# A layer with seven-product projections: the SSD cut into small pieces, loads ahead of use, two sums kept in SBUF

## The chip, the cores and the metric

The kernel runs on one core of a Trainium2 chip. The metric is device time in microseconds (us), the median of several runs. Engine names are those of the profile: PE multiplies matrices, DVE works element by element, ACT computes functions and scaled copies, POOL is a second element-wise engine, and SP issues nearly all DMA transfers. Each engine works through its own list of instructions in order.

## The reference

One layer of a decoder trunk with two branches behind one input projection and ahead of one output projection. The gMLP branch multiplies u, a spatially mixed v and a SiLU gate; the SSD branch is a depthwise convolution and a chunked state-space scan.

```python
def hybrid_layer(x, pre_w, w_in, v_norm_w, v_norm_b, ws, bs, gmlp_norm_w,
                 conv_w, conv_b, dt_bias, a_log, d_skip, ssd_norm_w, w_out, post_w):
    h = rms_norm(x, pre_w)                                   # x: 2048 x 1024
    proj = jnp.einsum('bld,dc->blc', h, w_in)                # w_in: 1024 x 6160
    u, v, zg, z, xbc, dt_raw = jnp.split(proj, SPLITS, axis=-1)
    y_a = spatial_gating(u, v, zg, v_norm_w, v_norm_b, ws, bs, gmlp_norm_w)
    y_b = ssd_mixer(xbc, z, dt_raw, conv_w, conv_b, dt_bias, a_log, d_skip, ssd_norm_w)
    mixed = jnp.einsum('blc,cd->bld', jnp.concatenate([y_a, y_b], axis=-1), w_out)
    return x + rms_norm(mixed, post_w)
...
def ssd_mixer(xbc, z, dt_raw, conv_w, conv_b, dt_bias, a_log, d_skip, norm_w):
    xbc = jax.nn.silu(causal_depthwise_conv(xbc, conv_w, conv_b))   # width 4
    xs, bm, cm = jnp.split(xbc, [SSD_WIDTH, SSD_WIDTH + SSD_GROUPS * D_STATE], axis=-1)
    ...
    decay = jnp.exp(jnp.where(causal, seg, -jnp.inf))        # per chunk of 128 and head
    cb = jnp.einsum('bclgn,bcsgn->bclsg', cm, bm)
    y_diag = jnp.einsum('bclsg,bclsgr,bcsgrp->bclgrp', cb, decay, xdt)
    states = jnp.einsum('bclgn,bclgr,bclgrp->bcgrpn', bm, decay_to_end, xdt)
    ...                                                      # state from chunk to chunk
    y_off = jnp.einsum('bclgn,bcgrpn,bclgr->bclgrp', cm, prev_states, jnp.exp(da_cs))
    y = (y_diag + y_off + xs * d).reshape(bsz, seq, SSD_WIDTH).astype(z.dtype)
    return grouped_rms_norm(y * jax.nn.silu(z), norm_w, SSD_WIDTH // SSD_GROUPS)
```

All is float32, with one sequence of 2048 positions and width 1024.

## The kernel before

**Tiling.** The sequence is cut into four blocks b of 512 positions. The input projection runs as six units of 1024 output columns (z, the two halves of xbc, v, and two halves of u with its gate), the output projection as unit 6. A unit uses Strassen's scheme in Winograd's form: blocks pair up as (0, 2) and (1, 3) (`PAIRS`), and for a pair seven products P1 to P7 take the place of eight. P1, P2 and P4 have a plain piece of the activations as their A operand, the others a sum: S3 for P7, S2 for P6, and one in P5 and P3; the weights have such sums (t3, t) as B operands. A finished operand is a 128x1024 float32 tile r, split into a rounded high part by ACT (line 158) and a rest by DVE (line 159). Three passes over the parts make up one product (`mm3`, lines 163 to 165).

**Steps.** A step is one product, one pair and one half or quarter j of the inner dimension: 24 products of 128x512 on four accumulators `acc`. A unit has 28 steps (`SETS` says which products come together; each set goes through both pairs), unit 6 has 56 (`ONES`), 224 in all. After the last j of a product, `after` adds the accumulator into the results in hand (tiles u, c), and `use_...` hands a finished result on: z through SiLU to DRAM, xbc to DRAM as `raw`, v with statistics, u into the gating, the last one into the output norm. Unit 0 stores its split A sums (`a_d`); units 1 to 5 load them as they are.

**What sets the order.** `look_ahead(i)` makes the operands of the steps up to i+3: loads, sums and split in one go. All other work is written as tasks, generators that issue a piece and yield. `run_tasks` runs after each accumulator's products and advances one task that is due. `issue_after` ties the piece to the step's last product, so pieces fall between steps on each engine. The SSD is one such task from unit 1 on: 16 blocks (b, group g), each a convolution of four 128x512 tiles (ACT line 341, DVE line 343 three times each, ACT line 344 with SiLU), transposes to `xtok` and `btok`, and four chunks. A chunk needs its decay matrix E (a load, four Relu and an Exp on ACT, lines 366 to 371), the operand xdt (DVE line 414) and products y_ps and st_ps (lines 428 to 433), then sums on DVE and POOL. Its state goes on to the next chunk. In units 4 and 5 the gMLP gating (`spatial`, `gate_in`, `gate_out`) runs beside it. `bring` loads what the last half of a row block needs for its output.

**Places.** The r tiles are a pool of six, A operands four, B operands five, and SSD and result tiles share `gpool` of 30. The sums S2 and S3 of units 0 and 6 go through DRAM (`s_d`): the P6 step stores S3 from tile t, then overwrites t with S2 and stores that; P7 and P3 load them back:

```python
        if name == "P6":
            t, q, r = load([piece(0, 0), piece(1, 0), piece(1, 1)])
            tt(t, t, q, ALU.subtract)
            nc.sync.dma_start(out=s_d[v, p, "S3", j], in_=t)
            tt(t, r, t, ALU.subtract)
            nc.sync.dma_start(out=s_d[v, p, "S2", j], in_=t)
```

## Time and profile before

| | us |
|---|---|
| median of 3 runs | 1740.42 (1739.19 to 1742.76) |
| the profiled execution | 1746.94 |
| its span, first to last instruction | 1745.2 |
| PE busy in it | 1564.6 (90%) |
| DVE, ACT, POOL busy | 1137.4, 908.9, 390.5 |

The times of the rows below are microseconds from the start of the span of the profiled execution. A busy PE is a PE with a product under way, not one at its peak, so the pace of steps is read from the times at which they begin. A wait is put down to what ended last.

### The profile page before, as it was taken

What the parts mean: (1) busy time and instruction counts of PE and PEld (TensorE: products, weight loads), DVE (VectorE), ACT (ScalarE), POOL (GpSimd) and SP (SyncE); (2) the same over time, 40 slices, a digit from 0 to 9 for tenths busy, and PEclk for the clock granted to TensorE, in tenths of its full rate; (3) what the DMA queues carried; (4) which work ended last, traced back from release to release, by engine and by line L of the source; (5) the groups of instructions that cost most, each with busy time, mean ns of one, the idle gap of its engine ahead of it and who ended that gap; (6) DMA issues with size and microseconds to landing.
All of it is one profiled execution on the core that took longest, in us unless ns stands there. A gap on an engine that the chain in (4) does not pass through costs nothing.

```text
span 1745.2 us, 21775 instructions
## 1 busy us (share of the span) xinstructions
PE 1564.6 (90%) x7268; PEld 1292.8 (74%) x7268; DVE 1137.4 (65%) x1748; ACT 908.9 (52%) x1849; POOL 390.5 (22%) x441
## 2 busy tenths in 40 slices
PE   4987889899989999799998889897899999699897
PEld 3866678788777778587886777786678888578786
DVE  4347666555675758747897558686547835666886
ACT  4332245553565656656565656978736852232332
POOL 1000000033033225422334233443332310000021
PEclk9977899999989999799998999998999999899998
DMA  9699998877777677586775676464756557998797
GB/s 332 225 356 351 373 410 287 331 239 264 267 262 260 238 274 246 190 279 260 268 261 191 220 258 242 153 195 154 290 203 255 182 175 259 376 334 272 264 388 281
DMA packets 161424, 465.28 MB, mean 267 GB/s; under 512 B 19104, under 2 KB 35872, under 8 KB 149024
## 3 DMA queue, kind: packets, MB, share of 16 engines
q1 hardware_dynamic: 161312, 463.89, 74.7%
q8 instruction: 57, 0.93, 0.2%
q14 instruction: 55, 0.45, 0.1%
HBM read 354.64 MB, written 109.18 MB: 266 GB/s over the span
## 4 chain that ended last, share of the span: by engine, by line
PE 46%; DMA 22%; DVE 14%; ACT 10%; issue 4%; POOL 2%; SPq 1%; DVEq 0%; ACTq 0%; POOLq 0%
PE acc L163 13%; PE acc L164 13%; PE acc L165 13%; DMA r<-w_u 5%; DMA r<-yd 3%; DVE cv_out L343 3%; PE y_ps L428 2%; DMA E<-scr 2%; DVE a L159 2%; ACT E L370 1%; DMA cv_raw<-raw 1%; DMA hd<-h 1%; DMA a<-as0P 1%; PE s_ps L505 1%; ACT L371 1%
## 5 line engine op out<-in xcount | busy, mean ns | idle before, releaser
L163 PE MATMUL acc<-b,a 128*128 128x512 f32 x1344 | 545.3, 412 | 78.5 <-ACT b L158 34.6
L164 PE MATMUL acc<-b,a 128*128 128x512 f32 x1344 | 544.4, 406 | 0.2
L165 PE MATMUL acc<-b,a 128*128 128x512 f32 x1344 | 533.4, 403 | 2.7 <-DVE a L159 2.7
L163 PEld LDWEIGHTS acc<-b,a 128*128 128x128 f32 x1344 | 262.4, 196 | 142.1 <-ACT b L158 36.9
L165 PEld LDWEIGHTS acc<-b,a 128*128 128x128 f32 x1344 | 261.4, 195 | 60.7 <-DVE a L159 4.3
L164 PEld LDWEIGHTS acc<-b,a 128*128 128x128 f32 x1344 | 263.1, 196 | 55.9 <-DVE b L159 1.8
L158 ACT ACTIVATE a<-r 128x1024 fp32r<-128x1024 f32 x144 | 151.2, 1054 | 230.3 <-PE acc L165 99.1
L159 DVE TENSOR_TENSOR a<-r,a 128x1024 fp32r<-128x1024 f32 x144 | 178.7, 1243 | 98.3 <-ACT a L158 94.4
L163 PE MATMUL acc<-a,b 128*128 128x512 f32 x448 | 180.5, 406 | 10.7 <-DVE u L728 3.1
L343 DVE SCALAR_TENSOR_TENSOR cv_out<-cv_raw,cw,cv_out 128x512 f32<-128x512 f32 x192 | 163.4, 865 | 29.2 <-ACT cv_out L341 27.6
L164 PE MATMUL acc<-a,b 128*128 128x512 f32 x448 | 179.4, 400 | 0.0
L165 PE MATMUL acc<-a,b 128*128 128x512 f32 x448 | 179.0, 401 | 0.0
L159 DVE TENSOR_TENSOR b<-r,b 128x1024 fp32r<-128x1024 f32 x112 | 139.4, 1247 | 54.9 <-ACT b L158 54.9
L158 ACT ACTIVATE b<-r 128x1024 fp32r<-128x1024 f32 x112 | 117.6, 1052 | 106.0 <-PE acc L165 38.7
L182 ACT ACTIVATE junk<-y 128x128 bf16<-128x128 f32 (+1 forms) x192 | 65.2, 340 | 127.6 <-POOL y L445 118.6
L416 POOL TENSOR_TENSOR xde<-xtok,dte 128x256 f32<-128x256 f32 x64 | 52.4, 818 | 315.8 <-ACT xtok L390 315.8
L163 PEld LDWEIGHTS acc<-a,b 128*128 128x128 f32 x448 | 85.9, 192 | 30.6 <-DVE u L728 3.5
L437 POOL TENSOR_TENSOR state<-state,ex 128x256 f32<-128x256 f32 x60 | 49.7, 828 | 258.4 <-PE y_ps L431 258.4
L370 ACT ACTIVATE E<-E,cs 128x128 f32<-128x128 f32 x256 | 79.4, 390 | 41.4 <-DMA E<-scr 38.7
L165 PEld LDWEIGHTS acc<-a,b 128*128 128x128 f32 x448 | 86.2, 192 | 18.2
L164 PEld LDWEIGHTS acc<-a,b 128*128 128x128 f32 x448 | 86.2, 192 | 17.5
L171 POOL TENSOR_TENSOR o_r<-o_ms,mhalf 128x1 f32<-128x1 f32 x16 | 16.9, 1059 | 318.7 <-DVE o_ms L169 290.2
(146 smaller groups left out, 2189.5 us busy)
## 6 DMA issues: line engine op xcount, KB each, us to landing
r<-w_u SPq DMA_DIRECT2D x108, 512.0 KB, 5.2
r<-hd SPq DMA_DIRECT2D x96, 512.0 KB, 5.9
a<-as0P SPq DMA_DIRECT2D x40, 1024.0 KB, 6.5
a<-as1P SPq DMA_DIRECT2D x40, 1024.0 KB, 7.0
r<-yd SPq DMA_DIRECT2D x72, 512.0 KB, 5.1
r<-w_o SPq DMA_DIRECT2D x44, 512.0 KB, 5.3
E<-scr SPq DMA_DIRECT2D x64, 256.0 KB, 5.3
yd<-yT SPq DMA_DIRECT2D x64, 256.0 KB, 2.8
```

Of the source, the lines that this page charges most:

```text
L158: nc.scalar.activation(w[:, :, 0, :], t, AF.Copy)
L159: nc.vector.tensor_tensor(w[:, :, 1, :], t, w[:, :, 0, :], ALU.subtract)
L163: nc.tensor.matmul(dst, lhsT=a_hi, rhs=b_hi, start=first, stop=False, skip_group_check=True)
L164: nc.tensor.matmul(dst, lhsT=a_hi, rhs=b_lo, start=False, stop=False, skip_group_check=True)
L165: return nc.tensor.matmul(dst, lhsT=a_lo, rhs=b_hi, start=False, stop=last, skip_group_check=True)
L182: nc.scalar.activation(junk[:, 0:n], src, AF.Square, accum_out=dst)
L343: nc.vector.scalar_tensor_tensor(cv, raw[:, j:j + T], cw[:, ti, j:j + 1], cv, ALU.mult, ALU.add)
L370: nc.scalar.activation(E[:, h, :], E[:, h, :], AF.Relu, scale=-1.0, bias=d["cs"][:, o + h:o + h + 1])
L371: nc.scalar.activation(E, E, AF.Exp, scale=-1.0)
L416: nc.gpsimd.tensor_tensor(h4(xde[:, :]), xc, hv(d["dte"], g, c), ALU.mult)
L428: nc.tensor.matmul(yps[:, h * HD:(h + 1) * HD], lhsT=E[:, h, :], rhs=xdt[:, h * HD:(h + 1) * HD], start=True, stop=True)
L437: nc.gpsimd.tensor_tensor(h4(st[:, :]), h4(st[:, :]), ev(d["ex"], 1, g, c), ALU.mult)
```

## The change

- **SSD pieces.** A class `Ssd` holds one block's tiles, and its methods are small pieces. While one block's chunks run, the next block's convolution goes one tile at a time between them, and the results of the block before are transposed and stored. Loads of raw, E and zs are issued at least one piece ahead of the piece that uses them. The task starts a few products into unit 1, rather than in its sixth step. With many tasks due, `run_tasks` advances more than one. `spatial` loads v a piece ahead too.
- **Loads ahead.** `make_a` and `make_b` are generators: the first part loads, one step ahead of the second, which sums and splits. This doesn't hold for the loads of the stored A operands and for the sums of unit 0. The A operands are made two steps ahead, from a pool of three; there are seven r and 32 g tiles.
- **S2 and S3.** In unit 0, S3 stays in its r tile until P7, and POOL copies S2 into two g tiles until P3. Unit 6 keeps its S2 and S3 in DRAM.
- **Orders.** Unit 0 is now the first half of xbc and unit 1 is z. In a unit P4 comes ahead of P5 and P3. In unit 6 the order is P1, P7, P2, P6, P4, P5, P3: P7 computes S3 and the weights' t3 and stores them, P6 loads them. P5 and P3 are now the products that finish a row's second half.

```diff
-LOOK_A = 3
+LOOK_A = 2
...
-SETS = (("P1", "P2"), ("P6", "P7"), ("P5", "P3"), ("P4",))
-ONES = tuple((m,) for m in PRODS)
+SETS = (("P1", "P2"), ("P6", "P7"), ("P4",), ("P5", "P3"))
+ONES = tuple((m,) for m in ("P1", "P7", "P2", "P6", "P4", "P5", "P3"))
...
-    apool = ctx.enter_context(tc.tile_pool(name="apool", bufs=4))
+    apool = ctx.enter_context(tc.tile_pool(name="apool", bufs=3))
-    rpool = ctx.enter_context(tc.tile_pool(name="rpool", bufs=6))
-    gpool = ctx.enter_context(tc.tile_pool(name="gpool", bufs=30))
+    rpool = ctx.enter_context(tc.tile_pool(name="rpool", bufs=7))
+    gpool = ctx.enter_context(tc.tile_pool(name="gpool", bufs=32))
...
-            advance(min(due, key=lambda t: t[0]))
+            for t in sorted(due, key=lambda t: t[0])[0:1 + len(due) // 4]:
+                advance(t)
...
+    def ssd_stream():
+        order = [(b, 2 * u + n) for u in range(2) for n in range(2) for b in range(NB)]
...
+        for n in range(len(order) + 1):
+            nxt = Ssd(*order[n + 1]) if n + 1 < len(order) else None
+            if nxt:
+                while not ready(nxt.b, nxt.g):
+                    yield 5
+            if cur:
+                while (cur.b, cur.g // 2) not in zs_in:
+                    yield 5
+                cur.load_e(0)
+                cur.load_e(1)
+                cur.tok_x(0)
+                yield 0
+                cur.tok_x(1)
+            if prev:
+                next(prev.out, None)
+            yield 0
+            if cur:
+                cur.tok_b()
+                cur.decay(0)
+                yield 0
...
+            for c in range(NT):
+                if nxt:
+                    nxt.conv(c)
+                    if c + 1 < NT:
+                        nxt.load_raw(c + 1)
+                if c + 2 < NT:
+                    cur.load_e(c + 2)
+                yield 0
+                if c + 1 < NT:
+                    cur.operands(c + 1)
+                cur.chunk(c)
+                if c + 2 < NT:
+                    cur.decay(c + 2)
+                    cur.load_z(c + 2)
+                yield 0
+            cur.norm()
+            yield 0
+            prev, cur = cur, nxt
...
-    UNITS = [(use_z(0), False, SETS, 2), (use_xbc(0), True, SETS, 2), (use_xbc(1), True, SETS, 2),
+    UNITS = [(use_xbc(0), True, SETS, 2), (use_z(0), False, SETS, 2), (use_xbc(1), True, SETS, 2),
...
     def make_a(u, p, name, j):
...
         if name in PLAIN_A:
-            return split(apool, "a", load([piece(*PLAIN_A[name])])[0])
+            t, = load([piece(*PLAIN_A[name])])
+            yield
+            yield split(apool, "a", t)
+            return
         if 0 < u < 6:
+            yield
             w = apool.tile([P, 2, 2, T], F32R, name="a")
             nc.sync.dma_start(out=w[:, :, :, :].bitcast(F32), in_=a_d[p][name, j][:, :, :, :])
...
+            if u == 0:
+                t, q, r = load([piece(0, 0), piece(1, 0), piece(1, 1)])
+                tt(t, t, q, ALU.subtract)
+                s3_in[p, j] = t
+                tt(r, r, t, ALU.subtract)
+                s2 = s2_in[p, j] = [gt("s2") for _ in range(2)]
+                for kk in range(2):
+                    nc.gpsimd.tensor_copy(s2[kk], r[:, kk, :])
+                t = r
+            else:
+                q, t = load([piece(1, 1), s_d[p, "S3", j]])
+                yield
+                tt(t, q, t, ALU.subtract)
+                nc.sync.dma_start(out=s_d[p, "S2", j], in_=t)
         elif name == "P7":
-            t, = load([s_d[v, p, "S3", j]])
+            if u == 0:
+                t = s3_in.pop((p, j))
+            else:
+                t, q = load([piece(0, 0), piece(1, 0)])
+                yield
+                tt(t, t, q, ALU.subtract)
+                nc.sync.dma_start(out=s_d[p, "S3", j], in_=t)
...
     def make_b(u, name, j):
...
+            else:
+                t, r = load([t3_d[j], piece(0, 0)])
+                yield
             tt(r, t, r, ALU.add)
             nc.sync.dma_start(out=t_d[u, j], in_=r)
...
                 t, q = load([piece(1, 1), piece(0, 1)])
+                yield
                 tt(t, t, q, ALU.subtract)
+                nc.sync.dma_start(out=t3_d[j], in_=t)
...
+        upto(2, i + LOOK_A, lambda *a: (load_a(*a) if looked[0] <= a[0] else None, do_a(*a),
+                                        looked.__setitem__(0, max(looked[0], a[0] + 1))))
+        upto(3, i + LOOK_B, lambda *a: (load_b(*a) if looked[1] <= a[0] else None, do_b(*a),
+                                        looked.__setitem__(1, max(looked[1], a[0] + 1))))
+        upto(0, i + LOOK_A + 1, load_a)
+        upto(1, i + LOOK_B + 1, load_b)
...
         elif name == "P6":
-            t["2"] = gt("u2")
-            tt(t["2"], t["3"], acc, ALU.add)
+            if alone:
+                t["2"] = t["1"]
+                tt(t["3"], t["3"], acc, ALU.add)
+            else:
+                t["2"] = gt("u2")
+            tt(t["2"], t["1"], acc, ALU.add)
...
-                spawn(ssd_stream(), 30)
+                spawn(ssd_stream(), 4)
...
-            if u == 6 and name in ("P3", "P4") and j == nj - 2:
-                bring(PAIRS[p][name == "P4"], c)
+            if u == 6 and name in ("P3", "P5") and j == nj - 2:
+                bring(PAIRS[p][name == "P5"], c)
```

On PE in unit 3, at the end of its fifth step. The rows are instructions in their order; acc are the steps' products, the others the small ones of the SSD. Before:

```order
L165 MATMUL acc_5536<-b_5489,a_5484 128x512
L428 MATMUL y_ps_5440<-xdt_5394,E_5218 128x64 x4
L431 MATMUL y_ps_5440<-state1_235,cv_out_5198 128x256
L433 MATMUL st_ps_5446<-xde_5396,btok_5307 128x256
L428 MATMUL y_ps_5513<-xdt_5467,E_5384 128x64 x4
L431 MATMUL y_ps_5513<-state1_235,cv_out_5198 128x256
L433 MATMUL st_ps_5519<-xde_5469,btok_5307 128x256
L428 MATMUL y_ps_5572<-xdt_5531,E_5457 128x64 x4
L431 MATMUL y_ps_5572<-state1_235,cv_out_5198 128x256
L433 MATMUL st_ps_5578<-xde_5533,btok_5307 128x256
L387 MATMUL xt_tp_5684<-ident_220,cv_out_5618 128x128 x2
L387 MATMUL xt_tp_5684<-ident_220,cv_out_5626 128x128 x2
```

Three chunks follow on one another there, and the next block's transposes behind them. On PE at a chunk in the same unit after the change:

```order
L166 MATMUL acc_5935<-b_5428,a_5780 128x512
L427 MATMUL y_ps_5818<-xdt_5743,E_5649 128x64 x4
L430 MATMUL y_ps_5818<-state1_231,cv_out_5382 128x256
L432 MATMUL st_ps_5824<-xde_5745,btok_5529 128x256
L164 MATMUL acc_5935<-b_5428,a_5780 128x512
L165 MATMUL acc_5935<-b_5428,a_5780 128x512
L166 MATMUL acc_5935<-b_5428,a_5780 128x512
```

A chunk now stands alone between the steps' products, and some 20 to 35 products lie between it and the next.

On SP's queue in unit 0, where the first P6 operands are made; r are loaded pieces, w_u the weights, hd and h the normalised input, zs1 the results of z. Before:

```order
L151 DMA r_774<-w_u 128x1024
L151 DMA r_776<-w_u 128x1024
L642 DMA s00S30_118<-r_758 128x1024
L248 DMA h_800<-x_t 128x1024
L151 DMA r_867<-hd0_1_85 128x1024
L555 DMA zs1_157<-stage_992 128x512
L555 DMA zs1_157<-stage_1001 128x512
L555 DMA zs1_157<-stage_1023 128x512
L671 DMA t00_140<-r_776 128x1024
L555 DMA zs1_157<-stage_1032 128x512
L644 DMA s00S20_116<-r_758 128x1024
```

The stores of S3 and S2 stand among the loads, the second behind the first. After:

```order
L152 DMA r_770<-w_u 128x1024
L250 DMA h_788<-x_t 128x1024
L152 DMA r_855<-hd0_0_84 128x1024
L152 DMA r_857<-hd2_0_92 128x1024
L152 DMA r_859<-hd2_2_94 128x1024
L771 DMA t01_137<-r_770 128x1024
L254 DMA hd2_3_95<-h_788 128x1024
L250 DMA h_906<-x_t 128x1024
L152 DMA r_961<-hd0_1_85 128x1024
L152 DMA r_963<-hd2_1_93 128x1024
L152 DMA r_965<-hd2_3_95 128x1024
```

The stores are gone from there; the loads for the weights' sums now stand ahead of the loads for S3 and S2.

On SP's queue in unit 6, the first P6 step before; yd are the branches' outputs, w_o the weights:

```order
L151 DMA r_12306<-yd0_4_184 128x1024
L151 DMA r_12308<-yd2_4_200 128x1024
L151 DMA r_12310<-yd2_0_196 128x1024
L642 DMA s60S30_128<-r_12306 128x1024
L151 DMA r_12319<-w_o 128x1024
L644 DMA s60S20_124<-r_12306 128x1024
L151 DMA r_12321<-w_o 128x1024
L151 DMA r_12323<-w_o 128x1024
```

And the first P7 step after the change, which now computes S3:

```order
L152 DMA r_12018<-yd0_4_180 128x1024
L152 DMA r_12020<-yd2_4_196 128x1024
L152 DMA r_12022<-w_o 128x1024
L528 DMA yd3_3_203<-yT_11876 128x512
L152 DMA r_12024<-w_o 128x1024
L733 DMA s0S30_120<-r_12018 128x1024
L152 DMA r_12060<-yd0_5_181 128x1024
```

Six loads and two of the step's stores became four loads and one store here, with the loads of the next step right behind.

## Rows read from the trace of the kernel before

**Rows 1.** The first part of the page: busy time, share of the span and instructions of each engine.

```profile
PE 1564.6 (90%) x7268; PEld 1292.8 (74%) x7268; DVE 1137.4 (65%) x1748; ACT 908.9 (52%) x1849; POOL 390.5 (22%) x441
```

**Rows 2.** The table of stretches, cut at the start of units 0 to 6. Columns: from:to, length, then busy us (and instructions) of PE, PE weight loads, DVE, ACT and POOL, mean granted clock, DMA share, GB/s.

```profile
42.00:280.60 238.60, 209.05 (x907) 169.92 (x908) 143.17 (x240) 88.27 (x134) 2.01 (x2) 0.89 0.91 343
280.60:464.20 183.60, 177.70 (x827) 147.18 (x826) 106.70 (x151) 86.82 (x146) 32.99 (x40) 0.98 0.78 274
464.20:683.50 219.30, 201.14 (x963) 166.82 (x962) 147.24 (x215) 134.15 (x245) 67.99 (x79) 0.96 0.73 256
683.50:905.10 221.60, 205.68 (x983) 170.50 (x982) 158.24 (x250) 128.60 (x242) 76.65 (x87) 0.95 0.72 251
905.10:1159.80 254.70, 225.80 (x1104) 187.80 (x1104) 175.85 (x304) 168.34 (x402) 99.44 (x112) 0.93 0.62 211
1159.80:1395.20 235.40, 212.23 (x1065) 177.38 (x1064) 155.05 (x266) 168.10 (x461) 82.75 (x90) 0.95 0.63 217
1395.20:1733.90 338.70, 316.98 (x1361) 258.93 (x1359) 225.39 (x272) 114.90 (x181) 19.36 (x17) 0.96 0.83 297
```

**Rows 3.** The same view, of two undisturbed stretches: eight steps of P7 in unit 6, and three steps with three chunks in unit 2.

```profile
1440.70:1484.20 43.50, 43.50 (x194) 36.02 (x193) 24.91 (x25) 12.60 (x18) 0.00 (x0) 1.00 0.75 262
605.50:627.20 21.70, 21.70 (x110) 18.48 (x108) 15.30 (x26) 5.65 (x12) 9.17 (x13) 1.00 0.83 311
```

**Rows 4.** The timeline, unit 0: start, length, engine, line, operation, count.

```profile
64.97 3.64 PE L256 MATMUL dt_ps<-wdt,h 128*128 128x16 f32 x32
```

**Rows 5.** The table of stretches, the first ten steps of units 1 to 5.

```profile
280.60:345.90 65.30, 60.37 (x262) 49.07 (x260) 32.91 (x39) 34.21 (x52) 4.16 (x3) 0.95 0.81 297
464.20:549.90 85.70, 73.67 (x345) 60.06 (x344) 52.59 (x71) 55.15 (x100) 23.00 (x27) 0.94 0.68 236
683.50:782.60 99.10, 85.29 (x394) 70.01 (x392) 60.19 (x89) 55.35 (x107) 37.30 (x43) 0.88 0.69 233
905.10:1011.40 106.30, 89.59 (x425) 73.96 (x424) 72.71 (x124) 63.46 (x141) 44.61 (x51) 0.89 0.65 219
1159.80:1268.50 108.70, 86.91 (x430) 71.54 (x428) 69.97 (x114) 89.85 (x235) 42.35 (x45) 0.91 0.64 220
```

**Rows 6.** The waits between 280 and 1395 us: who waited for what, us in total, times, the longest.

```profile
ACT cv_out L341 <- DMA cv_raw<-raw: 62.3, 24, 6.4
...
ACT E L370 <- DMA E<-scr: 38.7, 18, 5.3
...
PE y_ps L428 <- DVE xdt L414: 12.4, 5, 6.3
...
PE acc L163 <- DMA a<-as0P: 8.2, 4, 5.7
```

**Rows 7.** The timeline in unit 3; in brackets the idle time before and what ended it.

```profile
709.29 2.45 ACT L370 ACTIVATE E<-E,cs 128x128 f32<-128x128 f32 x8 [4.05 <-DMA E<-scr]
...
712.46 1.28 ACT L371 ACT_TABLE_LOAD   x1
713.76 1.15 ACT L371 ACTIVATE E<-E 128x512 f32<-128x512 f32 x2
...
724.20 3.08 DVE L343 SCALAR_TENSOR_TENSOR cv_out<-cv_raw,cw,cv_out 128x512 f32<-128x512 f32 x4
...
727.86 0.41 DVE L414 TENSOR_TENSOR xdt<-xtok,dt 128x256 f32<-128x256 f32 x1
...
728.42 1.94 PE L428 MATMUL y_ps<-xdt,E 128*128 128x64 f32 x8 [6.34 <-DVE xdt L414]
```

**Rows 8.** The table of stretches in unit 6: the eight P6 steps, the first P5 step of the second pair, and the last sixteen steps (P3 and P4).

```profile
1484.20:1552.10 67.90, 50.79 (x194) 39.72 (x193) 43.03 (x43) 15.18 (x21) 0.00 (x0) 0.87 0.96 360
1617.90:1630.30 12.40, 7.96 (x26) 6.05 (x25) 8.83 (x14) 3.68 (x10) 0.00 (x0) 0.73 0.64 219
1645.00:1734.00 89.00, 88.94 (x393) 73.31 (x391) 72.93 (x119) 30.57 (x55) 13.54 (x12) 1.00 0.95 353
```

**Rows 9.** The DMA view of unit 0 (42 to 280.6 us): the sum, and by tensor the count, KB each, us from issue to landing.

```profile
DMA packets 23819, 81.91 MB, mean 343 GB/s; under 512 B 2672, under 2 KB 3184, under 8 KB 21756
...
r<-s00S SPq DMA_DIRECT2D x4, 512.0 KB, 7.6
```

**Rows 10.** The timeline of the start.

```profile
34.43 5.36 SPq L151 DMA_DIRECT2D r<-w_u  x4
...
41.95 2.08 PE L163 MATMUL acc<-b,a 128*128 128x512 f32 x4 [10.44 <-ACT b L158]
```

**Rows 11.** The groups of instructions: line, engine, operation, count, busy us, mean ns, idle before.

```profile
L343 DVE SCALAR_TENSOR_TENSOR cv_out<-cv_raw,cw,cv_out 128x512 f32<-128x512 f32 x192 | 163.4, 865 | 29.2 <-ACT cv_out L341 27.6
```

**Rows 12.** The chain of waits in unit 6, in order of time: start, us, what.

```profile
1447.31 1.24 DVE r L641
...
1448.93 5.50 DMA s60S<-r
```

**Rows 13.** The DMA view of the whole span: the loads of the finished A operands.

```profile
a<-as0P SPq DMA_DIRECT2D x40, 1024.0 KB, 6.5
a<-as1P SPq DMA_DIRECT2D x40, 1024.0 KB, 7.0
```

**Rows 14.** The waits of SP's DMA queue between 280 and 1395 us.

```profile
SPq L635 <- PE acc L165: 168.1, 59, 12.3
```

More of the change, by code (lines that the diff above doesn't have):

```diff
@@ L328, in hybrid_kernel, with __init__, load_raw @@
     raw_in = set()
-    def conv(b, g, res):
-        for i in range(4):
-            ti = (2 * g, 2 * g + 1, 8 + g, 12 + g)[i]
-            raw = gfull("cv_raw")
+    zs_in = set()
+    class Ssd:
+        def __init__(self, b, g):
+            self.b, self.g, self.d = b, g, dts.get(b)
+            self.raw, self.cv, self.E, self.zs, self.ops, self.xtok, self.y = {}, {}, {}, {}, {}, {}, {}
+        def load_raw(self, i):
+            b, g = self.b, self.g
+            raw = self.raw[i] = gfull("cv_raw")
             if b:
@@ L413, in operands @@
+        def operands(self, c):
+            g, d = self.g, dts[self.b]
+            E = self.E[c]
+            nc.vector.tensor_tensor(E, E, self.cbm[:, c, :].unsqueeze(1).broadcast_to([P, HG, P]), ALU.mult)
+            xc = h4(self.xtok[c])
             xdt = qt("xdt")
@@ L418, in operands, with chunk @@
             nc.gpsimd.tensor_tensor(xc, xc, dsk, ALU.mult)
-            return E, xdt, xde
-        ops = operands(0)
-        yield 5
-        for c in range(NT):
-            E, xdt, xde = ops
+            self.ops[c] = xdt, xde
+        def chunk(self, c):
+            b, g, d, cT, st = self.b, self.g, dts[self.b], self.cv[3], state[self.g % 2]
+            xdt, xde = self.ops.pop(c)
+            E = self.E.pop(c)
             first = b == 0 and c == 0
@@ L721, in after @@
                 o = gt("c11")
[L722 removed]
+                tt(o, t["1"], acc, ALU.add)
                 use(m1, 0, c, o, False)
```

239 lines of the change are left out of this document (133 added, 106 removed).

## The prediction, made before the result was known

> **What bounds the kernel now.** The page's busy times come first [rows 1]: PE is busy 90% of the span, so the question is what keeps it from its pace. The table by unit [rows 2] cuts the span where units begin (each 672nd matrix product on acc). Then the pace: eight steps with nothing among them run in 43.5 us, 5.44 each; three steps with three SSD chunks among them take 21.7, so a chunk is (21.7 − 16.32)/3 = 1.79 [rows 3]; the other small products take 3.64/32 = 0.114 [rows 4]. A unit of 28 steps should take 152.3 us plus its small products (in the program's order 8, 16, 16, 16, 8 chunks and 60, 100, 120, 240, 296 others in units 1 to 5: 21.1, 40.0, 42.3, 56.0, 48.0 us). What lies above that is lost, most of it as PE waiting, the rest as a clock below 1.00: 10.2, 27.0, 27.0, 46.4 and 35.1 us in units 1 to 5 (145.7), 57 in unit 0 (29 us of small products there), 32.3 in unit 6 (304.6 + 1.8). The three kinds of unit lose for different reasons.
>
> Unit 0 is full of transfers: DMA share 0.91 at 343 GB/s [rows 2]. In units 1 to 5 the share is 0.62 to 0.78; there the first ten steps (P1 and P2, whose after-work hands two results per pair on while the B operands of a new unit are split) lose 8.6, 17.1, 23.7, 27.3, 31.1 us, by the same pace with 2.3, 14.2, 21.0, 24.6, 23.2 us of small products [rows 5]: 107.8 of the 145.7. The other 90 steps lose 37.9, or 0.42 each. In these stretches DVE is busy 50 to 68% of the time, ACT up to 83%: they are not full on average, but work comes in clumps. The waits say the same [rows 6]: PE waits little for any one thing (12.4 for xdt, 8.2 for an A load), while ACT, in order, stands 62.3 us for conv input and 38.7 for E, loads issued in the very piece that uses them; behind them on ACT's queue stand splits and evictions. One such place [rows 7]: ACT waits 4.05 for E at 709; four conv steps run on DVE from 724.20 to 727.28 ahead of xdt at 727.86, and PE waits 6.34 for it. Unit 6 loses 24.4 of its 32.3 in the eight P6 steps (67.9 against 43.5, DMA share 0.96) and 7 in one P5 step of 12.4 us [rows 8].
>
> **The change part by part.**
>
> Unit 0. S2 and S3 in SBUF remove 16 transfers of 512 KB (a store and a load of each, two pairs, two j) = 8.4 MB of 81.9 [rows 9]; at 343 GB/s 24 us. The wait of the second P6 subtraction for the S3 store goes too. Eight POOL copies come in; POOL is busy 2.01 us of 238.6 there, so they hide; without that cover they would cost some 9 us, at the 19.36/17 of a POOL instruction in unit 6 [rows 2]. Next late is the rest of the traffic (73.5 MB), and the share can't rise far over 0.91. If something else sets the unit's length, 0; at the 0.96 that unit 6's P6 reaches, 73.5 MB take 203 us, −35. I take three quarters of the 24: −18 (0 to −35).
>
> Start. SP issues four hd loads and behind them, from 34.43, the four w_u loads, 1.34 us each; PE's first product waits for the first B split and starts at 41.95 [rows 10]. Now the first w_u load goes right behind the first hd load, three issues or 4.0 us sooner, but the other A splits, ahead of it before, still have to be made: −3 (0 to −4).
>
> Units 1 to 5. Nothing here leaves the engines; it moves. On PE one chunk comes with each step where three chunks and eight transposes stood together; on DVE three conv steps between two chunks where twelve went, in two pieces, ahead of a block; loads of raw, E and zs one piece ahead, which takes up to 62.3 + 38.7 us of ACT's waits. Then a good stretch's rate should hold: the 30 opening steps of units 1 to 3 lose 49.4, at 0.42 each 12.6, so −37. In units 4 and 5 the same steps carry the spatial gating as well, DVE 72.7 and 70.0 us of work against 79.0 and 77.6 of PE's own, nine tenths: a queue that full can't absorb peaks, and I take half of their 58.4: −29. A loads now have one buffer less and two steps' lead in place of three, and SP meets them after more loads issued ahead: +4 (0 to the rival below). Together −62, between 0 and −88.
>
> Two costs for ACT and DVE. Mixing Silu of conv with Exp of decay piece by piece raises the table loads in ACT's order from 72 to 86. The row shows 1.28 us for one, and the next Exp starts 0.02 us behind it [rows 7]: 14 × 1.28 = 18 us on an engine busy 52%, spread over 1100 us, a wait for PE only where ACT is late; I put it inside the half of units 4 and 5. The Trainium skill ("ScalarE: Activation LUTs", What ACT_TABLE_LOAD costs) speaks against such an order: a switch of sets costs 1283 ns and a drain of some 1380 ns, 2.66 us. The row agrees on the load; of a drain this place shows none. By the page the 14 switches would be an estimated 37 us of ACT, still off the path by the busy share. Second, conv steps now run beside the chunks' POOL work. Four of them in a row take 3.08, 0.77 each, the mean of all 192 is 865 ns [rows 7, 11]. If that excess of 0.095 doubled, DVE would get 192 × 0.095 = 18 us more. The Trainium skill ("SBUF — State Buffer", Who interferes with whom) gives a reason: a DVE operation with two SBUF inputs and a GpSimd one lock each other out of a shared port. The rows fit that without showing it; what it adds is inside the range.
>
> Unit 6. Before, a P6 step loads three A pieces and stores S3 and S2, for the first pair it also loads three B pieces and stores t, and the second subtraction waits for the S3 store: 5.50 us from 1448.93 [rows 12]. That is 56 transfers, 29.4 MB. Now P7 and P6 have 18.9 MB each: 52.5 us at 360 GB/s against 43.5, with loads a step ahead in seven r tiles hiding half or more of the 9; I lose 4 in each: 24.4 to 8, −16. At the end P5 and P3 both carry final output: with 44 A and B loads (23.1 MB) where P3 and P4 had 36 (18.9). 353 GB/s over 89 us moved 31.4 MB [rows 8]; 4.2 more at 372 (353/0.95) make 95.5 us against 87: +8. Small rest −1. Sum −9, between +10 (P5 and P3 lose 20, DVE busy 72.9 of 89 there) and −20.
>
> Sum: −18 − 3 − 62 − 9 = −92. The profiled execution took 1746.94 (span 1745.2), 6.5 over the median of 1740.42; the losses are differences within it, and off the median the sum gives **1648**.
>
> **The rivals.**
>
> Units 1 to 5 gain nothing (0.20). The stalls come from DVE and ACT being too full in the opening steps, not from the clumps, or the tiles for loads ahead run short: the 32 g tiles must now hold one block's conv input and output beside the other's E, xtok, cbm and four to eight results, so a load ahead waits on SP for a tile and the rest of SP's queue behind it. For it: nine tenths of DVE in units 4 and 5. Against it: units 1 to 3, where DVE had 32.9 us of work against 56.7 and PE lost 8.6 all the same. Then 1648 + 62 = 1710.
>
> Slower: A operands come late (0.12). Three A buffers: a load may go out when the operand three steps back is used up, leaving two steps, 10.9 us, for SP to reach it and the transfer to land. Landing takes 6.5 to 7.0 [rows 13]; SP already waited 168.1 us in 59 pieces for such a buffer, up to 12.3 [rows 14], and everything issued behind it (E, raw, B halves) waits too. Before, with three steps, 4 of the 40 loads of as0P made PE wait, by up to 5.7 [rows 6, 13]. If every fourth of the 80 is late by 5.7, 20 × 5.7 = 114: 1648 + 114 = 1762. It decides from 92/5.7, about 16 late loads of all 80. Against it: 4 us of slack, and two steps become 14.5 with chunks.
>
> All of it works better (0.08): units 4 and 5 reach the good rate as well (58.4 to 8.4: another −21), unit 0 the full −24, unit 6 its −20: 1648 − 21 − 6 − 11 = 1610; if some of the 0.42 a step goes too, 1595.
>
> **How the numbers follow.** 0.60 for the forecast, spread by its bounds over some 1620 to 1685, 0.20 for 1710, 0.12 for late A operands, 0.08 for the best case. The range 1595 to 1722 takes in all but the slower rival and some tails. Faster by over 0.2% (3.5 us, about what a measurement of this kernel can tell from no change): 0.60 + 0.20 + 0.08 less some for cases between 1710 and 1740 that slip: 0.86. Within: 0.03. Slower: 0.11.
>
> **What would show it.** Unit 0 about 220 us long with 73.5 MB and the same share; its length unchanged at a lower share would say that compute or a buffer bounds it. The ten opening steps of units 1 to 3 losing about 4 us each, of 4 and 5 about 15; ACT's waits for cv_raw and E by DMA gone; xdt no longer a wait of several us on PE. If the late-A rival holds, PE's waits for `a<-as` stand first in the table and SP's for PE's acc grow. Unit 6: P7 and P6 about 47 us each, no wait of a subtraction for a store, P5 and P3 together about 95. The prediction is wrong where units 1 to 5 keep their losses though ACT's waits for loads are gone, since then a full queue, not a late load or a clump, set them.

## The result and the profile after

| | before | after |
|---|---|---|
| median, us | 1741.51 (1739.19 to 1742.76, 4 runs) | 1664.1 (1660.53 to 1670.95, 4 runs) |
| ratio to before | | 0.9562 (95% interval 0.9526 to 0.9597) |
| span of the profiled execution | 1745.2 | 1669.2 |

The kernel is 4.4% faster, 16 us slower than the 1648 that was forecast and inside the range. The table of stretches of the changed kernel, units 0 to 6, answers to [rows 2], with the same columns:

```profile
37.00:247.60 210.60, 199.70 (x907) 164.61 (x908) 142.48 (x250) 70.21 (x108) 7.19 (x10) 0.92 0.91 347
247.60:444.00 196.40, 187.75 (x891) 154.99 (x890) 131.42 (x187) 125.36 (x215) 47.86 (x58) 0.98 0.81 282
444.00:667.50 223.50, 204.62 (x990) 169.21 (x989) 146.37 (x222) 145.58 (x267) 75.83 (x89) 0.96 0.75 254
667.50:879.90 212.40, 201.29 (x969) 166.69 (x968) 158.36 (x254) 133.25 (x237) 66.15 (x79) 0.97 0.77 264
879.90:1104.30 224.40, 207.88 (x1040) 173.33 (x1039) 159.47 (x269) 162.70 (x372) 84.95 (x89) 0.97 0.66 225
1104.30:1345.90 241.60, 217.69 (x1053) 180.77 (x1052) 144.23 (x253) 160.21 (x448) 82.32 (x92) 0.91 0.60 205
1345.90:1656.50 310.60, 308.77 (x1361) 253.00 (x1359) 224.65 (x274) 114.68 (x179) 20.60 (x17) 1.00 0.89 321
```

Against the rows of before, unit 0 is 28.0 us shorter, the start 5.0 (42.0 to 37.0), units 1 to 5 together 16.3 (1114.6 to 1098.3), unit 6 28.1, and the tail behind it 1.4 longer: 76.0, all of the span's difference. Forecast were 18, 3, 62 and 9. The total came out within 16 us, its terms did not: units 1 to 5 gave a quarter of their share, unit 6 three times its own. So that the total lies near the forecast is in part luck: units 1 to 5 fell short by 46, and the other three terms gave 31 more than was forecast.

The opening ten steps of units 1 to 5 answer to [rows 5]:

```profile
247.60:308.60 61.00, 60.48 (x284) 49.87 (x283) 43.41 (x52) 36.24 (x57) 11.85 (x12) 1.00 0.90 311
444.00:539.60 95.60, 81.58 (x380) 65.87 (x378) 57.95 (x84) 66.25 (x121) 32.23 (x37) 0.91 0.68 224
667.50:750.30 82.80, 75.70 (x364) 61.79 (x363) 57.82 (x84) 55.04 (x95) 25.29 (x28) 0.96 0.73 247
879.90:976.30 96.40, 80.54 (x399) 65.75 (x397) 65.08 (x110) 65.42 (x151) 43.31 (x44) 0.96 0.64 220
1104.30:1228.40 124.10, 100.19 (x477) 81.95 (x475) 74.56 (x126) 95.08 (x258) 59.15 (x67) 0.85 0.60 203
```

By the prediction's count (5.44 us a step, 1.79 a chunk, 0.114 for another small product) they lose 1.2, 22.5, 11.6, 21.5 and 39.2 us: 96.0, where it was 107.8. The last row matters most: a clock of 0.85 over 124 us. The waits between 247 and 1346 us, against [rows 6]:

```profile
ACT cv_out L355 <- DMA cv_raw<-raw: 70.0, 34, 5.4
...
ACT E L371 <- DMA E<-scr: 31.7, 16, 6.9
...
PE acc L164 <- DMA a<-as1P: 11.9, 3, 9.8
...
PE y_ps L427 <- DVE E L410: 7.6, 3, 4.0
...
PE acc L164 <- DMA a<-as0P: 2.9, 4, 1.4
```

ACT still waits for raw and E, 101.7 us in all, where it was 101.0: issuing a load one piece ahead didn't shorten these waits in sum. A loads made PE wait 14.8 us in 7 places, not in twenty.

The products of unit 6, in the order P1, P7, P2, P6, P4, P5, P3, against [rows 8]:

```profile
1391.40:1436.40 45.00, 44.39 (x193) 35.77 (x192) 26.77 (x27) 15.07 (x17) 0.00 (x0) 1.00 0.87 324
...
1480.00:1523.50 43.50, 43.50 (x194) 36.02 (x193) 35.81 (x40) 14.55 (x20) 0.00 (x0) 1.00 0.99 372
...
1567.00:1611.10 44.10, 44.02 (x194) 35.82 (x193) 36.25 (x50) 16.83 (x27) 5.19 (x3) 1.00 0.95 345
1611.10:1656.50 45.40, 44.26 (x193) 35.68 (x191) 44.74 (x76) 14.19 (x26) 9.13 (x9) 1.00 1.03 390
```

P7, P6, P5 and P3 (the four rows) run at 45.0, 43.5, 44.1 and 45.4 us: PE never waits long, while the transfers reach 372 and 390 GB/s.

### The profile page after: what moved, and what is told of

Same layout as the page of the kernel before. It is cut to its first block, busy times and chain, and to the rows that moved or that the text cites. A ratio compares the mean times of both kernels' runs of the same rounds, so it can differ in the third digit from the quotient of the medians.

```text
span 1669.2 us, 21722 instructions
## 1 busy us (share of the span) xinstructions
PE 1543.6 (92%) x7268; PEld 1276.9 (76%) x7268; DVE 1129.3 (68%) x1756; ACT 929.3 (56%) x1863; POOL 394.5 (24%) x449
## 5 line engine op out<-in xcount | busy, mean ns | idle before, releaser
L164 PE MATMUL acc<-b,a 128*128 128x512 f32 x1344 | 544.4, 405 | 32.0 <-DMA a<-as1P 11.9
L165 PE MATMUL acc<-b,a 128*128 128x512 f32 x1344 | 534.6, 398 | 0.0
L166 PE MATMUL acc<-b,a 128*128 128x512 f32 x1344 | 526.1, 398 | 2.5 <-DVE a L160 1.7
L164 PEld LDWEIGHTS acc<-b,a 128*128 128x128 f32 x1344 | 257.0, 191 | 91.7 <-DMA a<-as1P 13.2
L166 PEld LDWEIGHTS acc<-b,a 128*128 128x128 f32 x1344 | 256.5, 191 | 60.0 <-DVE a L160 4.6
L165 PEld LDWEIGHTS acc<-b,a 128*128 128x128 f32 x1344 | 257.5, 192 | 51.0
L164 PE MATMUL acc<-a,b 128*128 128x512 f32 x448 | 182.4, 416 | 18.6 <-ACT a L159 4.7
L165 PE MATMUL acc<-a,b 128*128 128x512 f32 x448 | 184.3, 411 | 2.1 <-DVE a L160 2.0
L357 DVE SCALAR_TENSOR_TENSOR cv_out<-cv_raw,cw,cv_out 128x512 f32<-128x512 f32 x192 | 157.6, 832 | 37.5 <-ACT cv_out L355 36.0
L166 PE MATMUL acc<-a,b 128*128 128x512 f32 x448 | 181.6, 408 | 0.0
L164 PEld LDWEIGHTS acc<-a,b 128*128 128x128 f32 x448 | 87.9, 197 | 40.4 <-ACT a L159 6.1
L436 POOL TENSOR_TENSOR state<-state,ex 128x256 f32<-128x256 f32 x60 | 45.3, 756 | 274.6 <-PE y_ps L430 274.6
L165 PEld LDWEIGHTS acc<-a,b 128*128 128x128 f32 x448 | 88.7, 198 | 23.5 <-DVE a L160 5.2
L166 PEld LDWEIGHTS acc<-a,b 128*128 128x128 f32 x448 | 88.0, 196 | 19.2 <-issue 0.5
L355 ACT ACTIVATE cv_out<-cv_raw,cb,cw 128x512 f32<-128x512 f32 x64 | 51.9, 811 | 72.3 <-DMA cv_raw<-raw 70.0
L588 POOL TENSOR_TENSOR y<-y,sg 128x256 f32<-128x256 f32 x64 | 57.0, 903 | 145.0 <-ACT sg L587 132.8
```

The source lines that it names most:

```text
L164: nc.tensor.matmul(dst, lhsT=a_hi, rhs=b_hi, start=first, stop=False, skip_group_check=True)
L165: nc.tensor.matmul(dst, lhsT=a_hi, rhs=b_lo, start=False, stop=False, skip_group_check=True)
L166: return nc.tensor.matmul(dst, lhsT=a_lo, rhs=b_hi, start=False, stop=last, skip_group_check=True)
L355: nc.scalar.activation(cv, raw[:, 0:T], AF.Identity, scale=cw[:, ti, 0:1], bias=cb[:, ti:ti + 1])
L357: nc.vector.scalar_tensor_tensor(cv, raw[:, j:j + T], cw[:, ti, j:j + 1], cv, ALU.mult, ALU.add)
L436: nc.gpsimd.tensor_tensor(h4(st[:, :]), h4(st[:, :]), ev(d["ex"], 1, g, c), ALU.mult)
```

## The experiments

Each ran beside the kernel before; ratios are to that, with a 95% interval. "Loss" is the prediction's measure, from the profiled execution of each: the time from the first step of the units named to their end, less 5.44 us a step and the small products in it.

| kernel | median, us | ratio (interval) | loss, unit 0 | units 1 to 5 | unit 6 |
|---|---|---|---|---|---|
| before | 1741.5 | 1 | 57.0 | 145.7 | 32.3 |
| after | 1664.1 | 0.956 (0.953 to 0.960) | 29.0 | 129.0 | 4.1 |
| old_ssd | 1718.1 | 0.984 (0.980 to 0.988) | 31.3 | 183.2 | 0.6 |
| s_dram | 1681.8 | 0.965 (0.962 to 0.967) | 40.3 | 125.0 | 2.4 |
| u6_order | 1675.1 | 0.961 (0.960 to 0.963) | 25.4 | 121.1 | 19.7 |
| no_ahead | 1682.4 | 0.966 (0.963 to 0.968) | 43.3 | 123.6 | 4.0 |
| ssd_only | 1710.3 | 0.982 (0.979 to 0.985) | 51.3 | 119.5 | 28.5 |
| sets_old | 1662.1 | 0.954 (0.952 to 0.957) | 30.4 | 118.7 | 3.8 |
| no_loads | 1661.2 | 0.954 (0.951 to 0.957) | 24.9 | 120.9 | 5.0 |
| ps3 | 1641.3 | 0.942 (0.939 to 0.944) | 29.9 | 94.9 | 9.0 |
| before_ps3 | 1719.5 | 0.987 (0.983 to 0.991) | 53.1 | 126.8 | 25.5 |
| conv1 | 1655.3 | 0.949 (0.945 to 0.953) | 26.0 | 109.0 | 2.4 |
| ps3_sets | 1637.2 | 0.940 (0.936 to 0.943) | 32.0 | 87.8 | 8.0 |
| apool4 | 1690.0 | 0.970 (0.967 to 0.973) | 42.2 | 136.0 | 4.3 |

u6_order has the same code in units 0 to 5 as the changed kernel and the same order of products, and its losses there differ by 3.6 and 7.9 us. So differences of under some 10 us in units 1 to 5 are not read here. The losses are of one execution each: that of the changed kernel was the longest of its four, 6.9 us over the median, and that of s_dram the shortest, 6.5 under it.

The order of instructions is set when the program is built, and it moves with the pools and the work. In ps3, whose edit is two pool sizes, 1424 of the 1592 small products of the SSD and the gating stand behind another number of the steps' products than in the changed kernel, by up to 5.5 steps; conv1 and no_loads move them by up to 1.9 and 2.8. So each of these runs shows an edit together with the order that comes with it.

**old_ssd**: the changed kernel with the old stream.

```diff
-    UNITS = [(use_xbc(0), True, SETS, 2), (use_z(0), False, SETS, 2), (use_xbc(1), True, SETS, 2),
+    UNITS = [(use_z(0), False, SETS, 2), (use_xbc(0), True, SETS, 2), (use_xbc(1), True, SETS, 2),
...
-                spawn(ssd_stream(), 4)
+                spawn(ssd_stream(), 30)
```

(with `conv`, `ssd`, `ssd_stream`, `run_tasks` and the loads of `spatial` of before)

> The changed kernel with the SSD as it was before: one stream that does all four convolution tiles of a block, then its chunks, loads in the piece that uses them; z ahead of the first half of xbc; one task at a time; the v loads of the gating in the piece that uses them. Theory 1 (the pieces give what units 1 to 5 gained, 16 us): units 1 to 5 some 16 us longer, 1680 us. Rival (the pieces only move stalls from unit to unit, and something else gave the 16): within 5 us of 1664, with ACT's waits for raw and E about as large as in the changed kernel.

Measured: 54 us slower than the changed kernel, all of it in units 1 to 5. The pieces are worth more than theory 1 said, and the rival falls. But then the rest of the change costs the old stream 37.5 us there (183.2 against 145.7 before).

**ssd_only**: the reverse, the kernel before with the class `Ssd`, its unit order and `run_tasks` of after, and nothing else.

```diff
-            advance(min(due, key=lambda t: t[0]))
+            for t in sorted(due, key=lambda t: t[0])[0:1 + len(due) // 4]:
+                advance(t)
...
-                spawn(ssd_stream(), 30)
+                spawn(ssd_stream(), 4)
```

> The kernel before with the SSD in pieces alone: the class, the unit order with xbc first, tasks advanced by more than one; operands, pools, S2 and S3, product orders as before. In the changed kernel the old SSD stream cost 54 us, all of it in units 1 to 5, yet those units gained only 16 from before to after. Theory 1 (the pieces are worth some 54 anywhere, and another part costs units 1 to 5 some 38): 1742 - 54 = 1688. Rival (the pieces need P4 ahead of P5 and P3, which delivers their z and raw earlier, and are worth 16 without): 1725.

Measured: 1710, between the two. The loss of units 1 to 5 falls by 26, unit 0 by 6. So what the pieces give isn't one number: 26 us on the old operands, 54 on the new ones.

**s_dram**: S2 and S3 of unit 0 through DRAM.

```diff
-                s3_in[p, j] = t
-                tt(r, r, t, ALU.subtract)
+                nc.sync.dma_start(out=s0_d[p, "S3", j], in_=t)
+                tt(t, r, t, ALU.subtract)
+                nc.sync.dma_start(out=s0_d[p, "S2", j], in_=t)
```

> The changed kernel with S2 and S3 of unit 0 stored to DRAM and loaded back, as before. Theory 1 (unit 0 is bound by its bytes): the 8.4 MB come back at 347 GB/s, unit 0 takes 24 us more, near 235, and the kernel 1688. Rival (unit 0 gained from the store's wait and from the operands made ahead, not from bytes): the wait for the S3 store, some 5 us in four steps of unit 0, and partly hidden: 10 us, 1674.

Measured: unit 0 loses 11.3 us more in the profiled executions, near the rival's 10; by the medians the kernel is 17.7 us slower, midway between the rival's 1674 and theory 1's 1688. The row of unit 0 in that kernel, columns as in [rows 2]:

```profile
36.30:258.10 221.80, 202.62 (x906) 167.32 (x907) 143.67 (x247) 67.36 (x105) 2.01 (x2) 0.90 0.93 360
```

It moved its 80 MB at 360 GB/s where the changed kernel moved 73 at 347: transfers were not at their limit in the changed kernel's unit 0, and part of the time that the added bytes need went into that room.

**u6_order**: unit 6's products in the old order.

```diff
-ONES = tuple((m,) for m in ("P1", "P7", "P2", "P6", "P4", "P5", "P3"))
+ONES = tuple((m,) for m in ("P1", "P2", "P6", "P7", "P5", "P3", "P4"))
```

(and S3 and S2 both in P6, the weights' sum twice)

> The changed kernel with unit 6's products in the order of before (P1, P2, P6, P7, P5, P3, P4), S3 and S2 both made in P6 from three loads, the weights' sum made twice; loads stay a step ahead. Theory 1 (the order, which spreads the bytes and takes the store out of P6's chain, gave unit 6's 28 us): unit 6 near 335 us, the kernel 1688 to 1692. Rival (the loads a step ahead gave them): P6 loses under 8 us, the kernel below 1674.

Measured: unit 6 loses 19.7, between before (32.3) and after (4.1). The P6 steps in this kernel:

```profile
1422.60:1482.20 59.60, 50.29 (x193) 39.99 (x193) 42.25 (x44) 16.34 (x21) 0.00 (x0) 0.89 1.02 401
```

They take 59.6 us with the transfers at 401 GB/s, where before they took 67.9 at 360 [rows 8]. So with the old order the loads ahead take off 8 us; PE still loses 16 there, with the transfer engines full (share 1.02). By the medians the kernel is 11 us slower than the changed one, between theory 1 and the rival.

**no_ahead**: loads in the same go as their use, with the pools and lead of before.

```diff
-        upto(0, i + LOOK_A + 1, load_a)
-        upto(1, i + LOOK_B + 1, load_b)
```

(and LOOK_A 3, four A, six r and 30 g tiles)

> The changed kernel with the operand loads back in the same go as their sums and splits, A operands made three steps ahead from a pool of four, six r and 30 g tiles. Theory 1 (orders and bytes carry the gain, the loads ahead a third of unit 6's): unit 6 loses 8 us more, units 0 to 5 stay, 1672. Rival (loads ahead carry unit 6 and the good half of unit 0): unit 6 and unit 0 lose 30 us more together, 1694.

Measured: unit 6 loses 4.0, as in the changed kernel, so with the new order, and A operands made three steps ahead, loads ahead aren't needed there; both theories expected a loss. All that shows is unit 0: 14.3 us (18.3 by the medians of the whole).

**apool4**: four A buffers and a lead of three steps, with the loads ahead kept.

```diff
-LOOK_A = 2
+LOOK_A = 3
-        upto(0, i + LOOK_A + 1, load_a)
+        upto(0, i + LOOK_A + (i > 6), load_a)
```

(and four A, six r and 30 g tiles)

> The changed kernel with four A buffers, A operands made three steps ahead, six r and 30 g tiles; loads stay one step ahead but for the first steps of unit 0. PE waited 14.8 us in 7 pieces for loads of stored A operands in units 1 to 5. Theory 1 (a late A load is an accident of one or two places): 5 to 12 us faster, 1652 to 1659. Rival (the slower case of the prediction on a small scale: three buffers hold SP's queue, and what is issued behind is late too): 20 us or more, 1644 or less. Against both: two g tiles and one r tile less cost what it gives.

Measured: 26 us slower than the changed kernel by the medians, 20 in the profiled executions, 13 of that in unit 0; both theories fall, and what stands against both holds. PE's waits for A loads did shrink, from 14.8 to 6.5 us:

```profile
PE acc L164 <- DMA a<-as1P: 4.4, 2, 2.6
...
PE acc L164 <- DMA a<-as0P: 2.1, 2, 1.4
```

What it gave up for that weighs more: one r tile, two g tiles and the loads ahead of A in the first steps, which no_ahead lacks as well; these were not told apart.

**sets_old**: P4 behind P5 and P3 in units 0 to 5.

```diff
-SETS = (("P1", "P2"), ("P6", "P7"), ("P4",), ("P5", "P3"))
+SETS = (("P1", "P2"), ("P6", "P7"), ("P5", "P3"), ("P4",))
```

(and the start of the gating tasks and one result tile to match)

> The changed kernel with P4 behind P5 and P3 in units 0 to 5, as before, and the gating tasks started as long ahead of use as now. Theory 1 (the order of the sets is the part that costs units 1 to 5, since two products that hand on results now stand right ahead of the next unit's P1 and P2): 20 to 38 us faster, 1626 to 1644. Rival (the order helps, since z and raw of blocks 2 and 3 come sooner, and the cost is the loads ahead): slower, 1670 to 1690, the SSD waiting in unit 1 for z.

Measured: no difference (the intervals overlap), so neither theory holds. Units 1 to 3 lose 17.6 less (43.8 for 61.4); units 4 and 5 lose 7.3 more (74.9 for 67.6), which is within what is not read here.

**no_loads**: raw and E read from one constant tile.

```diff
-            raw = self.raw.pop(i)
+            raw = blank
...
-                nc.scalar.activation(E[:, h, :], E[:, h, :], AF.Relu, scale=-1.0,
+                nc.scalar.activation(E[:, h, :], blank[:, h * P:(h + 1) * P], AF.Relu, scale=-1.0,
```

(and 31 g tiles)

> The changed kernel without the loads of raw and E: convolution and decay read one constant tile, so their values are not the reference's, and 33 MB less is moved. ACT waited 70.0 us for raw and 31.7 for E. Theory 1 (late loads still make the stalls of units 1 to 5): their loss falls from 129 to under 95, the kernel below 1635. Rival (full queues and the two small PSUM banks make them): a loss of 115 or more, 1650 to 1664.

Measured: 1661, no difference to the changed kernel that the intervals show. ACT's 101.7 us of waits for these loads are gone, and others have grown. The first two of these rows are of the changed kernel, the others of no_loads:

```profile
ACT junk L183 <- POOL y L444: 47.5, 22, 5.7
ACT a L159 <- PE acc L166: 27.2, 13, 6.5
```

```profile
ACT junk L183 <- POOL y L438: 104.2, 33, 6.9
ACT a L159 <- PE acc L166: 62.4, 20, 8.6
```

These late loads are not what sets the time.

**conv1**: a third of the convolution's DVE work.

```diff
-            for j in range(1, 4):
+            for j in range(3, 4):
```

> The changed kernel with one of the three DVE steps of each convolution tile (two taps left out, so the values are not the reference's): 128 instructions of 832 ns, 106 us less on DVE. Theory 1 (the small banks, held from a product until DVE or ACT reads them, make the stalls, and a shorter DVE queue frees them only a little sooner): a fifth of the 129 us, 1636 to 1650. Rival (DVE's queue is too full in units 1 to 5): half of the loss goes, 1600 or less. Second rival (the order of instructions alone makes the stalls): within 8 us of 1664.

Measured: 1655, 9 us, from 95 us less DVE work in units 1 to 5 (644.7 us for 739.8). The loss falls by 20 in the profiled execution, the shortest of its four, but the medians' intervals overlap. That is between a fourteenth and a seventh of the loss for an eighth of DVE's work, between theory 1 and the second rival, and far from what a too full DVE queue would give back.

**ps3**: one PSUM bank moved to the small products.

```diff
-    pj = ctx.enter_context(tc.tile_pool(name="pj", bufs=6, space=PSUM))
-    ps = ctx.enter_context(tc.tile_pool(name="ps", bufs=2, space=PSUM))
+    pj = ctx.enter_context(tc.tile_pool(name="pj", bufs=5, space=PSUM))
+    ps = ctx.enter_context(tc.tile_pool(name="ps", bufs=3, space=PSUM))
```

> The changed kernel with three PSUM banks for the small products and five for the accumulators in place of two and six. Theory 1 (products wait for one of two small banks to be read: xt_tp 8.3 us, y_tp, s_ps and bt_tp some 15, and the clock falls behind each): units 1 to 5 lose 15 to 25 less, 1640 to 1650. Rival (the accumulators need the second spare bank, a step's first products then wait for an eviction): slower, 1680 to 1700.

Measured: 1641, theory 1. The profile of the changed kernel shows the largest place that it removed. In unit 5's third step PE runs 24 y_tp, 16 s_ps, three chunks and four xt_tp. The timeline of PE there, with the idle time ahead of each in brackets:

```profile
1133.55 0.66 PE L525 MATMUL y_tp<-ident,y 128*128 128x128 f32 x4 [1.82 <-DVE state L437]
1135.63 2.08 PE L566 MATMUL s_ps<-v,wsT 128*128 128x128 f32 x8 [1.42 <-ACT yT L527]
...
1141.91 2.08 PE L566 MATMUL s_ps<-v,wsT 128*128 128x128 f32 x8 [0.79 <-DVE state L437]
1144.52 1.12 PE L525 MATMUL y_tp<-ident,y 128*128 128x128 f32 x4 [0.53 <-DVE yo L442]
1146.83 1.09 PE L525 MATMUL y_tp<-ident,y 128*128 128x128 f32 x4 [1.20 <-DVE y L570]
...
1152.67 1.09 PE L525 MATMUL y_tp<-ident,y 128*128 128x128 f32 x4 [0.78 <-DVE yo L442]
1154.54 1.11 PE L384 MATMUL xt_tp<-ident,cv_out 128*128 128x128 f32 x4 [0.78 <-ACT yT L527]
```

Of the eight groups of y_tp, s_ps and xt_tp from 1133 on, seven wait for DVE or ACT to have read what one of the two banks still holds (the eighth and the chunks' own products don't). Two stretches of that step:

```profile
1124.50:1135.00 10.50, 7.89 (x33) 6.21 (x32) 8.41 (x12) 9.45 (x32) 6.60 (x9) 0.80 0.68 233
1135.00:1160.60 25.60, 20.80 (x73) 16.39 (x74) 14.57 (x29) 20.95 (x67) 14.75 (x17) 0.53 0.40 131
```

The waits are short, 0.5 to 1.8 us, 7.3 in all, but the clock is at 0.53 over the 25.6 us, so at its lower level (1.2 GHz) nearly all the time. An estimate of what the clock cost in the step's 36.1 us, from PE's busy time: 7.89 x 0.20 + 20.80 x 0.47 = 11.4. In ps3 unit 5 loses 11.3 us for 42.5, nearly the whole of the net gain, and over units 1 to 5 the clock rises from 0.96 to 0.98:

```profile
247.60:1345.90 1098.30, 1019.23 (x4937) 845.00 (x4936) 739.83 (x1182) 727.10 (x1534) 357.11 (x407) 0.96 0.71 244
```

```profile
248.40:1312.70 1064.30, 1004.70 (x4937) 831.18 (x4936) 746.47 (x1183) 724.91 (x1537) 374.48 (x407) 0.98 0.73 252
1113.60:1312.70 199.10, 192.05 (x965) 160.75 (x964) 122.39 (x211) 129.39 (x362) 63.02 (x67) 0.98 0.68 229
```

Units 1 to 5 are the first row of each kernel; the last row is unit 5 of ps3. Of the 34 us by which they differ, 19.5 are less idle time of PE (79.1 to 59.6, length less busy time); in the other 14.5 the same 4937 products are done in less busy time, which goes with the higher clock. PE's waits by kind, the first three rows from the changed kernel, the last two from ps3:

```profile
PE xt_tp L384 <- DVE yo L442: 8.3, 2, 4.9
PE s_ps L566 <- DVE state L437: 4.4, 2, 3.6
PE y_tp L525 <- ACT btok L397: 3.7, 1, 3.7
```

```profile
PE y_tp L525 <- ACT yT L527: 6.1, 3, 3.9
PE st_ps L432 <- DVE yo L442: 2.6, 5, 1.1
```

All rows of this kind, a small product behind a read of another one, come to some 30 us in the changed kernel and 14 in ps3. But the waits for A loads go too, from 14.8 to 1.0 us, and the order is another: the third step of unit 5 holds no small product in ps3 and takes 5.6 us. What the third bank gives with the order held was not tested, nor what made the A loads come in time.

**before_ps3**: the same two lines in the kernel before.

```diff
+    pj = ctx.enter_context(tc.tile_pool(name="pj", bufs=5, space=PSUM))
+    ps = ctx.enter_context(tc.tile_pool(name="ps", bufs=3, space=PSUM))
```

> The kernel before with three PSUM banks for the small products and five for the accumulators. In the changed kernel the third bank took 23 us. Theory 1 (two small banks bound the old stream as well: PE's waits ahead of small products are 61 of the 145.7 us lost in units 1 to 5, and the clock falls behind them): 25 us faster or more, 1717 or less. Rival (the old stream's clumps wait for DVE and ACT, and the pieces had to come first for a third bank to be of use): within 8 us, 1735 to 1742, or slower by the accumulators' missing bank.

Measured: 1719.5, 22 to 23 us: 2.5 short of theory 1's bound, and the rival falls. So the pieces needn't come first for a third bank, with its order, to be of use. Units 1 to 5 before and in before_ps3:

```profile
280.60:1395.20 1114.60, 1022.54 (x4937) 849.67 (x4936) 743.08 (x1182) 686.02 (x1493) 359.82 (x407) 0.95 0.69 239
```

```profile
275.10:1371.20 1096.10, 1013.73 (x4937) 842.25 (x4936) 739.99 (x1183) 680.08 (x1491) 362.87 (x409) 0.97 0.70 244
```

PE's waits for a bank fall from some 39 us to 17, while those for an accumulator to be read rise from 13 to 24, with one accumulator bank less; the idle time falls by 9.7 and the busy time by 8.8.

**ps3_sets**: ps3 and sets_old together.

```diff
+SETS = (("P1", "P2"), ("P6", "P7"), ("P5", "P3"), ("P4",))
...
+    pj = ctx.enter_context(tc.tile_pool(name="pj", bufs=5, space=PSUM))
+    ps = ctx.enter_context(tc.tile_pool(name="ps", bufs=3, space=PSUM))
```

> The changed kernel with three small PSUM banks and five for accumulators, and P4 behind P5 and P3 in units 0 to 5. The third bank alone gave 1641, with 12 us lost in unit 5 in place of 42; the old order of the sets alone lost 17 us less in units 1 to 3 and 17 more in unit 4. Theory 1 (the two gains are of different units and add up): 1620 to 1632. Rival (both take the same stalls away): 1636 to 1648.

Measured: 1637, in the rival's range, 4 us from ps3. In the profiled executions units 1 to 3 lose 44.4, as with sets_old alone (43.8; ps3 54.4), and units 4 and 5 lose 43.4, near ps3 alone (40.6). So the two gains are of different units, as theory 1 had it, but ps3 has 7 us of units 1 to 3 already and the sum stays short of theory 1's. It is the fastest kernel of the study, though its interval overlaps that of ps3.

## Why the prediction was right, point by point

**Units 1 to 5, the term that was wrong: 62 forecast, 16 measured.** The step that failed is the one that "a good stretch's rate should hold" once the clumps are spread and the loads come a piece ahead. Three things take it apart. Late loads, which the prediction read from ACT's 62.3 and 38.7 us, cost nothing: without them the time stays (no_loads). DVE being too full, the ground of the rival "units 1 to 5 gain nothing", is small (conv1). And clumps of chunks on PE were rare: in the kernel before, only two of the 48 pairs of neighbouring chunks of a block have no step's product between them, both in the place in unit 3 that was taken as the example; in the changed kernel it is two again, in unit 5's third step, where a chunk does not stand alone. What stayed in the way was not in the sum at all: two PSUM banks for all small products. PE's waits on them stood in the trace of before, each at a few us and under its own name. The waits of PE alone between 280 and 1395 us, kernel before:

```profile
PE y_tp L464 <- ACT xtok L390: 10.0, 4, 3.6
...
PE s_ps L505 <- DVE yo L443: 7.5, 3, 3.7
PE bt_tp L396 <- ACT yT L466: 6.8, 4, 2.8
...
PE s_ps L505 <- ACT yT L466: 4.6, 1, 4.6
...
PE xt_tp L387 <- DVE yo L443: 3.7, 4, 1.9
```

In each of these the releaser has read another small product, not made what this one needs: xtok is read from xt_tp, yo from y_ps, yT from y_tp. Together they are 32.6 of PE's 91.5 us, more than any wait for data; the prediction passed over them with "PE waits little for any one thing". ps3 and before_ps3 put a price of 22 to 23 us on one more bank and the order that comes with it, in either kernel; that the waits for a bank, and not the order, make this price is argued from their sums, not shown. Even so units 1 to 5 of ps3 still lose 94.9 us, and no run here takes that apart. The pieces alone are worth 26 us of units 1 to 5's loss, 54 on top of the rest of the change; the rest without them costs 37.5. Which of its parts does that to the old stream stays open; to the new one neither the order of the sets nor the lost A buffer costs anything that these runs can show.

The clock was named in one clause and priced nowhere. By the trace it stood at its lower level, 1.2 GHz, while PE was at work for 81 us of units 1 to 5 before and 76 after. Half of that is an estimate of what it cost: 40 and 38 us, over a quarter of their loss. In [rows 3] three chunks among steps ran at a clock of 1.00, and unit 5's third step, with as many and with waits, at 0.53 for most of it; no run tells whether the waits or the long row of small products hold it down.

**Unit 6, mis-sized: 9 forecast, 28 measured.** The mechanism held (bytes out of P6's set and the store out of its chain). The size failed in three places. P7 and P6 were charged as if most of their 18.9 MB each had to pass in their own 43.5 us; products that need few loads stand ahead of both, and by the rows only 14.6 and 16.2 MB moved in their own time, with 1.5 us lost where 8 were forecast. The end was charged 8 us more, where the transfers reached 390 GB/s and PE lost 2.5 (44.1 and 45.4 against 43.5), against 2.0 before. And the 7 us of the P5 step in [rows 8] were listed as a loss but not taken off; they are gone. The old order with loads ahead still loses 19.7, the new one without them 4.0: the order does it.

**Unit 0, a term missing: 18 forecast, 28 measured.** The 8.4 MB gave 11.3 by the profiled executions of s_dram and the changed kernel and 17.7 by their medians, so the 18 may be right and the full 24 is not seen. Some 14 came with the loads ahead or the pools that go with them (no_ahead, apool4), a term the sum didn't have.

**Start:** 3 forecast, 5.0 measured.

**The slower rival** (late A operands) didn't come: PE waited 14.8 us for them where it was 9.1 before, 5.7 more against the 4 in the sum, and a fourth buffer with what it displaces makes the kernel slower.

**ACT's table loads** rose to 86 as counted, 1283 ns each; no run here takes their cost apart. The convolution's mean on DVE went from 865 to 832 ns, where the prediction feared a rise: its steps now meet a POOL instruction less often, 95 of 192 for 105. Those that meet none take 746 ns in the mean in either kernel and 753 at most; those that meet one take 963 before and 919 after, up to 1241. The Trainium skill ("SBUF — State Buffer", Who interferes with whom) says that a DVE instruction with two SBUF inputs contends with a GpSimd one that reads SBUF; the trace agrees, with these numbers.

## What to carry to other kernels

Before spreading work to remove stalls, sum PE's short waits by what they have in common, not by name: here the largest sum was for a PSUM bank, and two lines gave 22 to 23 us in either kernel. Count how often a clump stands in the trace before taking one place as typical. When a pool's size changes, compare the order of instructions before giving the whole gain to the pool. A wait on an engine that isn't the bottleneck, even 100 us of it, says nothing until something takes it away. And products that need many bytes are best put between products that need few.
